# Gate and up of 18 of 22 feed-forward blocks as seven half-size block products, in a two-layer decoder trunk

## The chip, the cores and the metric

One Trainium2 chip, of which the kernel uses one core. The metric is the device time of one execution in microseconds (us), the median of several runs. PE is TensorE, PEld its weight load, DVE is VectorE, ACT is ScalarE, POOL is GpSimd, SP is SyncE.

## The reference

Two layers work on 544 positions at once (512 of a prompt and 8 samples of 4), model width 1024. Each layer has a mixer of four head groups (delta rule, short convolution, window attention, chunked token mixing) and then a feed-forward part of width 2816. Only the latter is touched by the change:

```python
x = x + jnp.concatenate([out_a, out_b, out_c, out_d], axis=-1) @ p['w_out']
h2 = rmsnorm(x, p['norm2_g'])
gate, f_conv_new = causal_dwconv(st['f_conv'], h2 @ p['ffn_w_gate'], p['ffn_conv_w'])
x = x + (jax.nn.silu(gate) * (h2 @ p['ffn_w_up'])) @ p['ffn_w_down']
```

The convolution runs over positions, width 3, each channel by itself. All is in float32.

## The kernel before

Activations lie with channels on the 128 partitions and the 544 positions along the free axis, so a tile of 128 channels is 128x544; `HT` is 272, half of the positions. Each float32 product is made of three: every operand is split into a high part, rounded to TensorE's fp32r format, and a low part, the remainder, and `gemm` (before L652) issues hi x hi, hi x lo, lo x hi for each of the k blocks of 128 channels, each for both halves of the positions: 6 matmuls of 128x272 for each block of 128x128 weights. TensorE's order is the program's own, which an `Order` object with side generators (the mixers) lays out; the other engines' queues are filled by a scheduler, earlier program text first among what is ready.

Weights come by `weights()` in the order of their use. `wload` issues the DMA of one weight tile (512 KB) on SP's queue into one of 2 buffers (`wrp`), `wprep` splits it: ScalarE copies the high part (L641), VectorE subtracts for the low part (L643), into 3 buffers each. `wnext` keeps three split tiles ready before it hands one out, so a tile is split when the buffer of the one three earlier has been given back by TensorE.

The feed-forward part (from L1553) goes through 22 blocks of 128 hidden channels, in groups of 6, 6, 6 and 4. In a block the gate product runs over the 8 k blocks (48 matmuls into PSUM tile `pgt`), then the up product (48 into `pup`); both take `xs`, the split of x times the norm's weight, which isn't yet divided by the root mean square. `rstd`, the reciprocal of that root, comes from the norm's own matmuls (`nps`) in the middle of the first up product, and multiplies the results: L1576 and L1577 on VectorE for the gate (into `pbf`, the buffer of the convolution), L1584 on GpSimd for the silu output `sl`. Then the convolution (`conv`: one ScalarE pass L694, two VectorE passes L696 into `cacc`), silu on ScalarE (L1582, L1583), the product with `pup` on VectorE (L1590), and the split into `hdh` and `hdl` (L499, L500). GpSimd also copies state in and out (`sfo`, L1578, L1579; L689). At the end of a group 8 down products (`pdn`, 36 matmuls in a group of 6, 24 in one of 4) take the group's hidden tiles, and VectorE adds each to the residual `xr` (L1600). The last two down products of the last layer are made half by half in `finale` (`pdl`), where each weight tile serves one half at a time.

```python
for wi, x in ((0, xh), (0, xl), (1, xh)):
    ...
    for j in range(2):
        mm(p[:, P0 + HT * j:P0 + HT * j + HT], w, x[:, HT * j:HT * j + HT],
           start=first, stop=last)
```

## Time and profile before

| | |
|---|---|
| median of 3 runs | 1376.19 us (1376.03 to 1376.20) |
| the profiled execution | 1375.83 us, of which the span from first to last instruction 1374.0 us |
| TensorE busy | 1343.9 us (98%), 12982 matmuls |
| VectorE, ScalarE, GpSimd busy | 777.2, 515.2, 292.2 us (57%, 37%, 21%) |
| granted TensorE clock | 0.99 |

The time outside the span is 1.8 us. Matmul spans overlap in the records, so the distance from one matmul to the next is read from a chain of many, not from one span.

### The profile page before, as it was taken

What the parts mean: (1) busy time and instruction counts of PE and PEld (TensorE: products, weight loads), DVE (VectorE), ACT (ScalarE), POOL (GpSimd) and SP (SyncE); (2) the same over time, 40 slices, a digit from 0 to 9 for tenths busy, and PEclk for the clock granted to TensorE, in tenths of its full rate; (3) what the DMA queues carried; (4) which work ended last, traced back from release to release, by engine and by line L of the source; (5) the groups of instructions that cost most, each with busy time, mean ns of one, the idle gap of its engine ahead of it and who ended that gap; (6) DMA issues with size and microseconds to landing.
All of it is one profiled execution on the core that took longest, in us unless ns stands there. A gap on an engine that the chain in (4) does not pass through costs nothing.

```text
span 1374.0 us, 30046 instructions
## 1 busy us (share of the span) xinstructions
PE 1343.9 (98%) x12982; PEld 1299.8 (95%) x12982; DVE 777.2 (57%) x1319; ACT 515.2 (37%) x852; POOL 292.2 (21%) x466
## 2 busy tenths in 40 slices
PE   8899999999999999999998999999999999999997
PEld 7888888999999999999998888989999999999997
DVE  5897944665445445435658977537444444444446
ACT  5446324443223223313534353335432332232234
POOL 2431220032103102203124311202320230121121
PEclk9899999999999999999999999999999999999999
DMA  6222241232232232232432222413223232322323
GB/s 224 89 83 72 82 133 43 82 113 77 81 106 79 76 107 80 74 106 67 140 120 79 78 82 62 138 52 87 92 81 89 93 85 80 98 89 71 103 68 96
DMA packets 48084, 125.62 MB, mean 91 GB/s; under 512 B 10144, under 2 KB 14432, under 8 KB 47824
## 3 DMA queue, kind: packets, MB, share of 16 engines
q1 hardware_dynamic: 47952, 123.70, 29.6%
q8 instruction: 102, 1.67, 0.5%
q14 instruction: 30, 0.25, 0.1%
HBM read 115.01 MB, written 8.67 MB: 90 GB/s over the span
## 4 chain that ended last, share of the span: by engine, by line
PE 88%; DVE 8%; issue 2%; ACT 1%; DMA 0%; DVEq 0%; SPq 0%; ACTq 0%
PE pup L417 19%; PE pgt L417 19%; PE pdn L417 19%; PE po L417 7%; PE ptm L417 2%; PE pj_b L417 2%; PE pj_z L417 2%; PE pj_u L417 2%; PE pj_h L417 2%; PE pj_cq L417 2%; PE pj_c L417 2%; PE p L417 2%; PE pj_v L417 1%; DVE wl L643 1%; DVE cacc L696 1%
## 5 line engine op out<-in xcount | busy, mean ns | idle before, releaser
L641 ACT ACTIVATE wh<-wr 128x1024 fp32r<-128x1024 f32 (+3 forms) x218 | 208.5, 957 | 502.0 <-PE pdn L417 177.2
L643 DVE TENSOR_TENSOR wl<-wr,wh 128x1024 fp32r<-128x1024 f32 (+3 forms) x218 | 246.2, 1129 | 24.2 <-ACT wh L641 18.3
L417 PE MATMUL pgt<-xl,wh 128*128 128x272 f32 x704 | 146.7, 290 | 0.0
L417 PE MATMUL pup<-xl,wh 128*128 128x272 f32 x704 | 146.7, 290 | 0.0
L417 PE MATMUL pup<-xh,wl 128*128 128x272 f32 x704 | 145.9, 289 | 0.0
L417 PE MATMUL pgt<-xh,wl 128*128 128x272 f32 x704 | 145.9, 289 | 0.0
L417 PE MATMUL pup<-xh,wh 128*128 128x272 f32 x704 | 145.9, 288 | 0.0
L417 PE MATMUL pgt<-xh,wh 128*128 128x272 f32 x704 | 145.9, 288 | 0.0
L417 PE MATMUL pdn<-hdl,wh 128*128 128x272 f32 x688 | 142.8, 289 | 0.0
L417 PE MATMUL pdn<-hdh,wh 128*128 128x272 f32 x688 | 142.4, 288 | 0.0
L417 PE MATMUL pdn<-hdh,wl 128*128 128x272 f32 x688 | 142.2, 288 | 0.0
L1600 DVE TENSOR_TENSOR xr<-xr,pdn 128x544 f32<-128x544 f32 x62 | 44.7, 721 | 142.0 <-PE pdn L417 141.8
L1578 POOL COPY sfo<-pbf 128x2 f32<-128x2 f32 x44 | 14.8, 336 | 517.9 <-DVE pbf L1576 517.9
L1576 DVE TENSOR_TENSOR pbf<-pgt,rstd 128x512 f32<-128x512 f32 x44 | 30.5, 693 | 148.3 <-PE pgt L417 142.9
L417 PEld LDWEIGHTS pgt<-xh,wh 128*128 128x128 f32 x704 | 110.8, 188 | 0.0
L417 PEld LDWEIGHTS pup<-xh,wh 128*128 128x128 f32 x704 | 110.8, 188 | 0.0
L417 PEld LDWEIGHTS pup<-xl,wh 128*128 128x128 f32 x704 | 110.7, 189 | 0.0
L417 PEld LDWEIGHTS pgt<-xl,wh 128*128 128x128 f32 x704 | 110.7, 189 | 0.0
L417 PEld LDWEIGHTS pgt<-xh,wl 128*128 128x128 f32 x704 | 110.7, 188 | 0.0
L417 PEld LDWEIGHTS pup<-xh,wl 128*128 128x128 f32 x704 | 110.7, 188 | 0.0
L417 PEld LDWEIGHTS pdn<-hdl,wh 128*128 128x128 f32 x688 | 108.1, 188 | 0.1
L417 PEld LDWEIGHTS pdn<-hdh,wl 128*128 128x128 f32 x688 | 108.1, 188 | 0.0
(523 smaller groups left out, 2680.0 us busy)
## 6 DMA issues: line engine op xcount, KB each, us to landing
wr<-w_g SPq DMA_DIRECT2D x44, 512.0 KB
wr<-w_u SPq DMA_DIRECT2D x44, 512.0 KB
wr<-w_ch SPq DMA_DIRECT2D x38, 512.0 KB
wr<-w_d SPq DMA_DIRECT2D x48, 384.0 KB
wr<-w_o SPq DMA_DIRECT2D x12, 384.0 KB
wr<-w_d SPq DMA_DIRECT2D x16, 256.0 KB
xr<-x_in SPq DMA_DIRECT2D x7, 544.0 KB
wr<-w_tm SPq DMA_DIRECT2D x8, 392.0 KB
```

The lines of the kernel that those rows point to most:

```text
L417: nc.tensor.matmul(out, lhsT, rhs, **kw)
L641: act(hi, r, AF.Copy)
L643: tt(lo, r, hi.bitcast(F32), op=ALU.subtract)
L696: stt(acc[:, 0:out_n], pb[:, j:j + out_n], wcol[:, j:j + 1], acc[:, 0:out_n], op0=ALU.mult, op1=ALU.add)
L1576: tt(pb[:, 2:2 + SEQ], pflat(p, 0, SEQ), rstd[:, 0:SEQ], op=ALU.mult)
L1578: pool.tensor_copy(sfo[:, f, 0:2], pb[:, SEQ:SEQ + 2])
L1600: tt(xk(m), xk(m), pflat(p), op=ALU.add)
```

## The change

The 1024 input channels and the 544 positions are each cut in half, and the gate and up weights are taken as the two rows of a 2x2 block matrix. The product of a 2x2 block matrix (gate and up by the two halves of the channels) with a 2x2 block matrix (the two halves of the channels by the two halves of the positions) is made from seven block products in place of eight, with sums of blocks on both sides. Each block product runs over 4 k blocks, in the same three terms, one half of the positions: 12 matmuls of 128x272 (`chain`).

- Sums of weights: `wsums`, four GpSimd additions of 128x512 for each hidden block, in two tiles `s12` and `s43`. The tiles to split are then gate, `s12`, `s43` (1024 wide each) and the second half of up (512 wide). Four raw weight buffers in place of two, plus two for the sums.
- Sums of activations: `Forms`. `halves` makes the normed input (x times weight times `rstd`) and splits its halves; `sums` makes and splits the four sums. Both are made once in each layer.
- Blocks 0 and 1 stay as they were (`raw`); blocks 2 and 3 are plain products on the split normed input (`plain`), where ScalarE copies the gate to `pbf` with no factor; blocks 4 to 21 are made by `seven`. Only `raw` still multiplies by `rstd`.
- In `seven` partial results stay in PSUM across chains: a chain with start=False adds to what ScalarE has copied out to `sn` before.
- Groups are 4, 6, 6, 6, and the down products of a group are spread among the blocks of the next one (after the blocks of a group of six: 2, 2, 2, 1, 1, 0); those of the last group follow at the end.
- The pools `hlp`, `lv`, `px` and `pyy` become one pool of 51 buffers.

```diff
-FGROUPS = [(0, 6), (6, 12), (12, 18), (18, 22)]
+FGROUPS = [(0, 4), (4, 10), (10, 16), (16, 22)]
+RAW, PLAIN = 2, 4
...
+def _ffn_order():
+    o, todo = [], []
+    for f0, f1 in FGROUPS:
+        n = f1 - f0
+        for j, f in enumerate(range(f0, f1)):
+            o.append(("plain" if f < PLAIN else "seven", f, f0, f1))
+            k = -(-len(todo) // max(n - 1 - j, 1))
+            o += todo[:k]
+            todo = todo[k:]
+        o += todo
+        todo = [("down", m, f0, f1) for m in range(NK)]
+    return o + todo
...
+FFN_ORDER = _ffn_order()
...
-    hlp = ctx.enter_context(tc.tile_pool(name="hlp", bufs=28))
-    wrp = ctx.enter_context(tc.tile_pool(name="wrp", bufs=2))
+    slabs = ctx.enter_context(tc.tile_pool(name="slabs", bufs=51))
+    wrp = ctx.enter_context(tc.tile_pool(name="wrp", bufs=4))
+    wsp = ctx.enter_context(tc.tile_pool(name="wsp", bufs=2))
     whp = ctx.enter_context(tc.tile_pool(name="whp", bufs=3))
     wlp = ctx.enter_context(tc.tile_pool(name="wlp", bufs=3))
     p5 = ctx.enter_context(tc.tile_pool(name="p5", bufs=6))
-    lv = ctx.enter_context(tc.tile_pool(name="lv", bufs=1))
     pd = ctx.enter_context(tc.tile_pool(name="pd", bufs=5))
-    px = ctx.enter_context(tc.tile_pool(name="px", bufs=16))
-    pyy = ctx.enter_context(tc.tile_pool(name="pyy", bufs=5))
     pc = ctx.enter_context(tc.tile_pool(name="pc", bufs=7))
...
+    class Forms:
...
+        def __init__(self, src):
+            self.src, self.got, self.h = src, [], []
+            self.hv = [slice(HT * i, HT * i + HT) for i in range(2)]
+        def halves(self, kp):
+            h = []
+            for k in (kp, kp + NK // 2):
+                x, g = self.src(k)
+                t = nx("hn", [128, T])
+                stt(t, x, g, rstd, op0=ALU.mult, op1=ALU.mult)
+                h.append(t)
+            j = kp % 2
+            if j == 0:
+                self.pk = [[nx(f"f{i}" + c, [128, T], F32R) for c in "hl"] for i in "12"]
+            c_ = slice(HT * j, HT * j + HT)
+            one = []
+            for (hi, lo), v in zip(self.pk, (h[0][:, 0:HT], h[0][:, HT:T])):
+                act(hi[:, c_], v, AF.Copy)
+                tt(lo[:, c_], v, hi[:, c_].bitcast(F32), op=ALU.subtract)
+                one.append((hi[:, c_], lo[:, c_]))
+            sb = split(h[1], "f3")
+            self.got.append(one + [(sb[0][:, s], sb[1][:, s]) for s in self.hv])
+            self.h.append(h)
+        def sums(self, kp):
+            h, self.h[kp] = self.h[kp], None
+            (b11, b12), (b21, b22) = ((t[:, 0:HT], t[:, HT:T]) for t in h)
+            u, v = n5("fu", T), n5("fv", T)
+            n1, n2, t3, n4 = u[:, 0:HT], u[:, HT:T], v[:, 0:HT], v[:, HT:T]
+            tt(n1, b11, b12, op=ALU.subtract)
+            stt(n2, n1, -1.0, b22, op0=ALU.mult, op1=ALU.subtract)
+            tt(t3, b22, b12, op=ALU.subtract)
+            tt(n4, b21, n2, op=ALU.add)
+            for t in (split(u, "f4"), split(v, "f5")):
+                self.got[kp] += [(t[0][:, s], t[1][:, s]) for s in self.hv]
...
+        def whole(self):
+            return [(kp + NK // 2 * i, g[2 * i:2 * i + 2]) for kp, g in enumerate(self.got) for i in range(2)]
+        def parts(self):
+            return [[g[i] for g in self.got] for i in (0, 2, 3, 4, 5, 6, 7)]
+    def chain(o, wt, k0, xs, start=True):
+        hi, lo = wt
+        n = len(xs)
+        for k in range(n):
+            xh, xl = xs[k]
+            for i, (w, x) in enumerate(((hi, xh), (hi, xl), (lo, xh))):
+                mm(o, w[:, k0 + k, :], x, start=start and k == 0 and i == 0, stop=k == n - 1 and i == 2,
+                   skip_group_check=not start)
+            yield 0.0
...
+            for kind, i, f0, f1 in FFN_ORDER:
+                if kind == "down":
+                    yield I["w_d"][l, i, :, f0:f1], f1 - f0, 128
+                elif kind == "plain":
+                    yield I["w_g"][l, i], NK, 128
+                    yield I["w_u"][l, i], NK, 128
+                else:
+                    yield I["w_g"][l, i], I["w_u"][l, i]
...
+    wload_, wsplit_, wready = [], [], []
...
-            wload_.append(r)
+            wload_.append([wraw(*x)] if len(x) == 3 else [wraw(src, NK, 128) for src in x])
+    def wsums(g, u):
+        K = NK // 2
+        lo_, hi_ = slice(0, K), slice(K, NK)
+        s12 = wsp.tile([128, NK, 128], F32, tag="ws", name="s12")
+        s43 = wsp.tile([128, NK, 128], F32, tag="ws", name="s43")
+        add = pool.tensor_tensor
+        add(s12[:, lo_], u[:, lo_], u[:, hi_], op=ALU.add)
+        add(s12[:, hi_], g[:, lo_], s12[:, lo_], op=ALU.add)
+        add(s43[:, lo_], g[:, hi_], s12[:, hi_], op=ALU.add)
+        add(s43[:, hi_], g[:, lo_], u[:, lo_], op=ALU.add)
+        return [g, s12, s43, u[:, hi_]]
...
+        if not wsplit_:
+            if not wload_:
+                wload()
+            if not wload_:
+                return
+            rs_ = wload_.pop(0)
+            wsplit_.extend(rs_ if len(rs_) == 1 else wsums(*rs_))
+        r = wsplit_.pop(0)
...
+    def gemm_halves(p, wt, xs):
+        for n, (k, x) in enumerate(xs):
+            for i, (w, c) in enumerate(((0, 0), (0, 1), (1, 0))):
+                for j in range(2):
+                    mm(p[:, P0 + HT * j:P0 + HT * j + HT], wt[w][:, k, :], x[j][c],
+                       start=n == 0 and i == 0, stop=n == NK - 1 and i == 2)
+            if n < NK - 1:
                 yield 0.0
...
+            hid = {}
+            fm = Forms(lambda k: (xk(k), P(l, "n2g", k, k + 1)))
...
+            def raw(f, first):
+                p = psmm("pgt")
+                yield from gemm(p, wnext(), xs)
+                pu = psmm("pup")
...
+                pool.tensor_tensor(sl, sl, rstd, op=ALU.mult)
+                yield 0.0
+                yield from gu
+                tt(sl, sl, pflat(pu), op=ALU.mult)
+                hid[f] = split(sl, "hd")
+                yield 0.0
...
+            def plain(f):
+                p = psmm("pgt")
+                yield from gemm_halves(p, wnext(), fm.whole())
+                pb, dec = gate_in(f)
+                act(pb[:, 2:2 + SEQ], pflat(p, 0, SEQ), AF.Copy)
+                act(dec[:, :, 2:6], bs(pflat(p, SEQ, T)), AF.Copy)
+                sl = gate_out(f, pb, dec)
+                yield 0.0
+                pu = psmm("pup")
+                yield from gemm_halves(pu, wnext(), fm.whole())
+                tt(sl, sl, pflat(pu), op=ALU.mult)
+                hid[f] = split(sl, "hd")
+                yield 0.0
+            def seven(f):
...
+                B11, B21, B22, N1, N2, T3, N4 = fm.parts()
+                K = NK // 2
+                a_ = ps("pA", [128, HT])
+                b_ = psa.tile([128, HT], F32, tag="pa1", name="pB")
+                d_ = psa.tile([128, HT], F32, tag="pa0", name="pD")
+                sn = pd.tile([128, 4, HT], F32, tag="d5", name="sn")
+                pb, dec = gate_in(f)
+                n = SEQ - HT
+                w = wnext()
+                yield from chain(a_, w, 0, B11)
+                act(sn[:, 0], a_, AF.Copy)
+                yield from chain(b_, w, K, B21)
+                tt(pb[:, 2:2 + HT], b_, sn[:, 0], op=ALU.add)
+                w = wnext()
+                yield from chain(d_, w, 0, N1)
+                act(sn[:, 1], d_, AF.Copy)
+                yield from chain(a_, w, K, N2, start=False)
+                act(sn[:, 2], a_, AF.Copy)
+                w = wnext()
+                yield from chain(d_, w, 0, B22, start=False)
+                tt(pb[:, 2 + HT:2 + SEQ], d_[:, 0:n], sn[:, 2, 0:n], op=ALU.add)
+                tt(dec[:, :, 2:6], bs(d_[:, n:HT]), bs(sn[:, 2, n:HT]), op=ALU.add)
+                sl = gate_out(f, pb, dec)
+                yield from chain(a_, w, K, T3, start=False)
+                act(sn[:, 3], a_, AF.Copy)
+                up = n5("up", T)
+                stt(up[:, HT:T], a_, -1.0, sn[:, 1], op0=ALU.mult, op1=ALU.subtract)
+                c_ = psmm("pC")[:, 0:HT]
+                yield from chain(c_, wnext(), 0, N4)
+                tt(up[:, 0:HT], c_, sn[:, 3], op=ALU.subtract)
+                tt(sl, sl, up, op=ALU.mult)
+                hid[f] = split(sl, "hd")
+                yield 0.0
...
+            for kind, i, f0, f1 in FFN_ORDER:
+                if kind == "plain":
+                    yield from raw(i, i == 0) if i < RAW else plain(i)
+                    if i == 0:
+                        for kp in range(NK // 2):
+                            fm.halves(kp)
+                    elif i < 3:
+                        fm.sums(2 * i - 2)
+                        fm.sums(2 * i - 1)
+                    continue
+                if kind == "seven":
+                    yield from seven(i)
+                    continue
+                m, last = i, f1 == NF
+                hd = [hid[f] for f in range(f0, f1)]
+                if last and l + 1 == depth and m >= NK - 2:
...
+                p = psmm("pdn")
+                yield from gemm(p, wnext(), hd)
+                tt(xk(m), xk(m), pflat(p), op=ALU.add)
...
+    nc = _bacc.Bacc("TRN2", target_bir_lowering=False, num_devices=1, dynamic_dma_scratch_size=512)
```

## Rows read from the trace of the kernel before

**Rows 1.** The page, part 1: busy us, share of the span, instructions.
```profile
PE 1343.9 (98%) x12982; PEld 1299.8 (95%) x12982; DVE 777.2 (57%) x1319; ACT 515.2 (37%) x852; POOL 292.2 (21%) x466
```

**Rows 2.** The page, part 4: shares of the chain that ended last.
```profile
PE 88%; DVE 8%; issue 2%; ACT 1%; DMA 0%; DVEq 0%; SPq 0%; ACTq 0%
```

**Rows 3.** The chain that ended last, in time: start us, us, what.
```profile
285.35 6.08 PE pgt L417 x48
...
297.97 6.08 PE pgt L417 x48
...
358.77 36.37 PE pdn L417 x288
...
1357.46 4.53 PE pdl L417 x36
```

**Rows 4.** Busy time in stretches: length, each engine, then granted clock, DMA.
```profile
285.30:334.40 49.10, 49.10 (x390) 49.10 (x389) 25.06 (x33) 20.90 (x31) 15.84 (x22) 1.00 0.27 92
...
1012.60:1339.00 326.40, 326.40 (x2593) 326.40 (x2592) 147.37 (x192) 96.51 (x132) 59.81 (x88) 1.00 0.29 85
```

**Rows 5.** VectorE groups by form: busy us, mean ns, idle before.
```profile
L643 DVE TENSOR_TENSOR wl<-wr,wh 128x1024 fp32r<-128x1024 f32 x132 | 167.9, 1272 | 19.8 <-ACT wh L641 13.9
...
L696 DVE SCALAR_TENSOR_TENSOR cacc<-pbf,prm,cacc 128x560 f32<-128x560 f32 x88 | 70.4, 800 | 4.0 <-ACT cacc L694 2.3
...
L643 DVE TENSOR_TENSOR wl<-wr,wh 128x768 fp32r<-128x768 f32 x60 | 57.1, 951 | 0.0
...
L1590 DVE TENSOR_TENSOR sl<-sl,pup 128x544 f32<-128x544 f32 x44 | 31.8, 722 | 111.0 <-PE pup L417 103.1 <-POOL sl L1584 7.9
...
L500 DVE TENSOR_TENSOR hdl<-sl,hdh 128x544 fp32r<-128x544 f32 x44 | 31.6, 719 | 0.5
...
L643 DVE TENSOR_TENSOR wl<-wr,wh 128x512 fp32r<-128x512 f32 x18 | 12.3, 684 | 0.0
```

**Rows 6.** VectorE instructions of line 547 and of line 596: min/median/max ns.
```profile
L547 DVE SCALAR_TENSOR_TENSOR xl<-xr,prm,xh x32: 772/784/1886, 5.5 to 965.8; 128x544 fp32r<-128x544 f32 x32
...
L596 DVE TENSOR_TENSOR sq<-sq x2: 439/441/443, 1361.1 to 1363.0; 128x272 f32<-128x272 f32 x2
```

**Rows 7.** Timeline of VectorE, gate and up of layer 0.
```profile
296.47 0.69 DVE L1576 TENSOR_TENSOR pbf<-pgt,rstd 128x512 f32<-128x512 f32 x1 [2.73 <-ACT rstd L541]
```

**Rows 8.** ScalarE groups by form.
```profile
L641 ACT ACTIVATE wh<-wr 128x1024 fp32r<-128x1024 f32 x132 | 139.6, 1058 | 313.9 <-PE pgt L417 142.1 <-PE pdn L417 63.9 <-PE pup L417 27.3
...
L641 ACT ACTIVATE wh<-wr 128x512 fp32r<-128x512 f32 x18 | 11.4, 632 | 26.6 <-PE pgt L417 8.7 <-PE pup L417 6.2 <-PE pdn L417 5.7
...
L1253 ACT ACTIVATE oc<-pov 128x256 f32<-128x256 f32 x8 | 3.0, 380 | 6.0 <-PE pov L417 6.0
```

**Rows 9.** GpSimd instructions of four lines: min/median/max ns.
```profile
L841 POOL TENSOR_TENSOR Gu<-cst,gg x4: 1043/1046/1046, 61.6 to 789.0; 128x512 f32<-128x512 f32 x4
...
L1102 POOL TENSOR_TENSOR s<-s,ex x4: 1045/1544/1917, 165.0 to 835.6; 128x512 f32<-128x512 f32 x4
...
L1579 POOL COPY sfo<-pbf x44: 190/1243/1250, 297.3 to 1334.6; 128x16 f32<-128x16 f32 x44
...
L1584 POOL TENSOR_TENSOR sl<-sl,rstd x44: 1354/1359/1367, 301.1 to 1337.4; 128x544 f32<-128x544 f32 x44
```

**Rows 10.** Timelines of VectorE and of GpSimd at 511 us.
```profile
511.31 1.23 DVE L643 TENSOR_TENSOR wl<-wr,wh 128x1024 fp32r<-128x1024 f32 x1
...
511.35 1.24 POOL L1579 COPY sfo<-pbf 128x16 f32<-128x16 f32 x1
```

**Rows 11.** Busy time in stretches of 2 us, layer 1.
```profile
726.00:728.00 2.00, 0.00 (x0) 0.00 (x0) 1.97 (x8) 0.24 (x1) 0.05 (x1) 1.00 0.19 68
...
728.00:730.00 2.00, 0.00 (x0) 0.00 (x0) 1.94 (x6) 1.73 (x4) 1.46 (x5) 0.65 0.00 0
...
732.00:734.00 2.00, 2.00 (x10) 2.00 (x11) 2.00 (x5) 0.02 (x1) 0.00 (x0) 0.50 0.66 172
```

More of the change, by code (lines that the diff above doesn't have):

```diff
@@ L451, in n5, with nx @@
         return p5.tile([128, w], F32, tag="w5", name=nm)
-    def nx(nm, shape):
-        return px.tile(shape, F32, tag="x5", name=nm)
+    def nx(nm, shape, dt=F32):
+        return slabs.tile(shape, dt, tag="s5", name=nm)
     def ncc(nm, shape):
@@ L459, in ny @@
     def ny(nm, shape):
-        return pyy.tile(shape, F32, tag="y5", name=nm)
+        return nx(nm, shape)
     def ps(nm, shape):
@@ L615, in weights, with wraw @@
                 yield I["w_o3"][l, m], NK, 128
-            for f0, f1 in FGROUPS:
-                for f in range(f0, f1):
-                    yield I["w_g"][l, f], NK, 128
-                    yield I["w_u"][l, f], NK, 128
-                for m in range(NK):
-                    yield I["w_d"][l, m, :, f0:f1], f1 - f0, 128
-    wgen = weights()
-    wload_, wready = [], []
+            for kind, i, f0, f1 in FFN_ORDER:
[6 more added lines that the diff above has]
+                    yield I["w_g"][l, i], I["w_u"][l, i]
+    wgen = weights()
+    wload_, wsplit_, wready = [], [], []
+    def wraw(src, nk, w):
+        r = wrp.tile([128, nk, w], F32, tag="wr", name="wr")
+        nc.sync.dma_start(r, src)
+        return r
     def wload():
@@ L786, in gates @@
         L.beta, L.nbeta, L.gg, L.ex, L.bec = beta, nbeta, gg, ex, bec
-        L.oT = [lv.tile([128, T], F32, tag=f"oT{pr}", name=f"oT{pr}") for pr in range(2)]
+        L.oT = [nx(f"oT{pr}", [128, T]) for pr in range(2)]
         od.mark(f"gates{l}", 1.0)
     def halves(x):
-        h = hlp.tile([128, SEQ], F32R, tag="hl", name="hvh")
-        lo = hlp.tile([128, SEQ], F32R, tag="hl", name="hvl")
+        h, lo = nx("hvh", [128, SEQ], F32R), nx("hvl", [128, SEQ], F32R)
         act(h, x, AF.Copy)
@@ new lines, in main, with gate_in, gate_out @@
+            hid = {}
+            fm = Forms(lambda k: (xk(k), P(l, "n2g", k, k + 1)))
+            def gate_in(f):
+                pb = n5("pbf")
+                return pb, conv_in(pb, 3, stf[:, f])
+            def gate_out(f, pb, dec):
+                pool.tensor_copy(sfo[:, f, 0:2], pb[:, SEQ:SEQ + 2])
+                pool.tensor_copy(sfo[:, f, 2:18].rearrange("p (b s) -> p b s", b=DB), dec[:, :, 4:6])
+                acc, accd = conv(pb, 3, P(l, "fcw", 3 * f, 3 * f + 3), 560)
+                sl = n5("sl", T)
+                act(sl[:, 0:SEQ], acc[:, 0:SEQ], AF.Silu)
+                act(bs(sl[:, SEQ:T]), accd, AF.Silu)
+                return sl
@@ new lines, in raw @@
+            def raw(f, first):
+                p = psmm("pgt")
+                yield from gemm(p, wnext(), xs)
+                pu = psmm("pup")
+                gu = gemm(pu, wnext(), xs)
+                if first:
+                    for _ in range(4):
+                        yield next(gu)
+                    nrm.finish()
+                pb, dec = gate_in(f)
+                tt(pb[:, 2:2 + SEQ], pflat(p, 0, SEQ), rstd[:, 0:SEQ], op=ALU.mult)
+                tt(dec[:, :, 2:6], bs(pflat(p, SEQ, T)), bs(rstd[:, SEQ:T]), op=ALU.mult)
+                sl = gate_out(f, pb, dec)
[5 more added lines that the diff above has]
+                yield 0.0
@@ new lines, in main @@
+            for kind, i, f0, f1 in FFN_ORDER:
[14 more added lines that the diff above has]
+                if last and l + 1 == depth and m >= NK - 2:
+                    if m == NK - 2:
+                        yield from finale(xk, xr, nnrm, hd)
+                    continue
+                p = psmm("pdn")
+                yield from gemm(p, wnext(), hd)
+                tt(xk(m), xk(m), pflat(p), op=ALU.add)
+                if last:
+                    if l + 1 < depth:
+                        nx_xs.append(xsplit(xk(m), P(l + 1, "n1g", m, m + 1)))
+                    nnrm.feed(m, xk(m))
+                    if l + 1 == depth:
+                        act(xk(m), xk(m), AF.Copy, scale=fng[:, m:m + 1])
+                yield 0.0
```

67 lines of the change are left out of this document (6 added, 61 removed).

## The prediction

> **What bounds the kernel now.** I read the page's busy table first [rows 1]: TensorE is busy 98% of the span, VectorE 57%, ScalarE 37%, GpSimd 21%. Then the shares of the chain that ended last [rows 2]: PE 88%, VectorE 8%. So the kernel is a queue of matmuls, with its gaps elsewhere. Then the same chain in time [rows 3], to see what the feed-forward part is made of: 48 matmuls of a gate or an up product stand as one piece of 6.08 us, the next piece begins where the last one ended, and 288 matmuls of the down products take 36.37 us. There is no wait between them. The stretches agree [rows 4]: from 285.3 to 334.4 us (four blocks at the start of layer 0) and from 1012.6 to 1339.0 us (most of layer 1's part) TensorE is busy for all of the time at granted clock 1.00, and VectorE for 51% and 45% of it. What matters is therefore how many matmuls there are, how far apart they stand, and whether the other engines, which get more work, still keep ahead.
>
> **Matmuls removed.** A block costs 96 matmuls now; seven chains of 12 make 84. That is 12 less in 18 blocks of 2 layers: 432. A piece of 48 gives 6.08/48 = 126.7 ns from one to the next. The new chains use a weight tile for one half of the positions at a time, which the gate and up products never do, but the last two down products do: 36 in 4.53 us are 125.8 ns [rows 3], so this form costs no more. At 126.2 ns, 432 matmuls are **54.5 us**. Blocks 0 to 3, the down products and the norms keep their counts, and regrouping the downs moves them without changing their number. From here all other terms are losses, for whatever hides work cannot shorten a queue that has no gap.
>
> **Steady blocks: the load.** TensorE has 84 x 126.2 ns = 10.6 us for a block. VectorE: the weight tiles to split become 3.5 of the 1024 kind for 2, that is 3 x 1.23 [rows 10] + 0.68 [rows 5] = 4.4 us; the two convolution passes 1.6; product and hidden split 1.44 [rows 5]; and four half-width additions from PSUM, taken as 0.44 each by the nearest row [rows 6], 1.8: together 9.2 us. GpSimd: four additions of 128x512, 1.05 us each when nothing is in the way and up to 1.92 [rows 9], 4.2 us; three small copies at 0.19, 0.6; the 1.36 us product with `rstd` falls away. ScalarE gains 1.06 + 0.63 for splits and 4 copies from PSUM at about 0.38 [rows 8], 3.2 us a block, on a queue that is 30% busy here [rows 4]; hidden. Over a group of six with its 8 downs, TensorE has 6 x 10.6 + 36.4 = 100 us, VectorE 6 x 9.2 + 8 x (0.95 + 0.72) = 69 us, GpSimd 29 us. On average both fit.
>
> **Where the two collide.** In the timelines a GpSimd copy of 128x16 begins 0.04 us after a VectorE split of 1.23 us and ends 0.05 us after it [rows 10]; alone such a copy takes 0.19 us, and 1.24 is its median [rows 9]. So a GpSimd operation that reads SBUF waits out a VectorE operation with two SBUF inputs; line 547's maximum of 1.89 us against a median of 0.78 [rows 6] is the same thing the other way round. The Trainium skill (SBUF — State Buffer, Who interferes with whom) says that the two fully exclude each other for a whole instruction, which speaks against putting the sums on GpSimd. By that rule the losses below stand at their upper ends, some 46 us in all, and without it near their lower ones; the trace agrees with the rule in the rows just named.
>
> If nothing overlaps, a group needs 69 + 29 = 98 us of 100. But the downs are not spread evenly: the last block of a group has none behind it, and the first of the next has none ahead, so twice a layer two blocks stand together: 21.2 us of TensorE against 2 x 9.2 (full overlap) to 2 x (9.2 + 4.8) = 28.0 us (none). On top come the splits of up to three hidden blocks (3 x 0.72 = 2.2 us): the 51 buffers less 32 for the forms of the input and 2 for states leave 17, so from the third block of a group the hidden tiles wait for the old group's last down. Two weight tiles are split ahead, of 24 matmuls or 3.0 us each; one of them I count as cover. Bounds for each of the 4 places: 0 to 28.0 + 2.2 - 21.2 - 3.0 = 6.0 us. I take 1.5, near the lower end, since half-width operations with a PSUM input can run beside GpSimd: **6 us** in all.
>
> **The start of each feed-forward part.** `rstd` arrives about 11.2 us after the first gate product starts (296.47 against 285.35 [rows 7, 3]). Only then can VectorE make the forms: for each of 4 pairs, two scalings at 0.78, two half-width subtractions at 0.44, one of 0.72 [rows 5, 6], 3.16 us, 12.6 in all; and four sums at 0.44 and two subtractions at 0.72, 3.2 us, 12.8 in all. They are due when block 2 and the third chain of block 4 start, at 24.8 and 52.1 us. VectorE is busy 25 of the first 49 us today [rows 4], 4.7 of it before `rstd` (one addition 0.72, two splits 2.46, two low parts 0.78 and 0.72); two gate scalings go to ScalarE (1.7 less). So after `rstd` it has 25.1 - 4.7 - 1.7 + 25.4 = 44 us of work in 41. GpSimd adds its 2 x 1.36, 4.2 of sums and eight copies at 0.19, 8.4 us, all in the way if nothing overlaps. Loss for a layer: 0 (the operations can be a little closer than their spans) to 3 + 8 = 11 us; I take 5, between them, as VectorE's queue has no room to catch up here: **10 us** in two layers. Queued behind the forms on VectorE are the splits of block 2's weights and the scaling of block 1's gate, which gives back the PSUM tile that block 2 needs; so the wait will show at block 2 and block 4.
>
> **Waits inside a block.** The third chain's tile (D) is copied out by ScalarE while the fourth chain runs, 12 matmuls or 1.51 us, before the fifth adds to it; likewise A between its second and third use. The copy is 0.38, so 1.1 us is left for what stands ahead of it. One split (1.06) just fits; two would hold TensorE by 1.0 us. Bounds 0 to 1.0 at each of two places; I take 0.03, as the queue is free two thirds of the time: **2 us** over 36 blocks. `sn` has one buffer (four of five hold `xr`); its writer waits for the last addition of the block before, with 3 us in hand.
>
> **At nothing.** Weight loads: SP issues two at a time into four buffers, the same bytes, at a DMA share of 0.29 [rows 4]. What is queued behind them on SP are only loads that are due later. The longer last down products (36 in place of 24 matmuls) give the norm of the next layer more cover, not less. The common pool can let a mixer run earlier or wait; nothing in the trace prices it, bounds plus or minus 2 us, 0 taken.
>
> **The sum.** The profiled execution took 1375.83 us, its span 1374.0; 1374.0 - 54.5 + 10 + 6 + 2 = 1337.5, with 1.8 outside it 1339.3. The median is 0.4 above that execution: **1339.7 us**.
>
> **Rivals.** (a) *Clean.* VectorE's slack holds and the forms come in time: losses up to 7 us, 1321.7 to 1328. For it: VectorE idles over half of these stretches. Against: the 44 us in 41 after `rstd`. Chance 0.2. (b) *The forecast*, waits at the starts and at group ends, 1328 to 1352: 0.52. (c) *GpSimd and VectorE shut each other out all through*: starts at 11, ends at 6.0, 22 + 24 = 46 us, so 1368; with part of it, or a little beyond, 1352 to 1372. It is the rule of the Trainium skill's page SBUF — State Buffer, Who interferes with whom, taken at its word. For it the copy that waited out the split; against it the room in blocks with downs. Chance 0.2. (d) *Slower*: the copies of D and A reach ScalarE's queue behind a split that itself waits for GpSimd's sums, so TensorE stops twice in each block. At the 1.0 us bound this is 36 x 2 x 1.0 = 72 us, 1394; from 0.76 us a place it outweighs the 54.5. A stop of that kind can also cost the clock: after TensorE did nothing from 726 to 730 us the granted clock read 0.50, the lower of its two levels, until after 734 [rows 11]. Against it: the sums have a whole block's time, and ScalarE is 30% busy. Chance 0.08 with (e), no measurable change, at 0.02. That the matmuls would not fall in number is excluded by the count, and that they would stand further apart by the row of the last down products [rows 3].
>
> **How the numbers follow.** Most likely is (b) at its sum, 1339.7. The range 1324 to 1364 leaves out about 0.05 of (a) at its floor, 0.06 of (c), and (d) and (e). About 0.2% (2.8 us) is what a measurement of this kernel can tell from no change. Faster 0.92, within it 0.02, slower 0.06.
>
> **What would show it.** Right: pieces of 12 matmuls at 1.51 us in the chain; 432 fewer matmuls; waits of TensorE on VectorE of a few us at block 2 and block 4 of each layer, and next to none in blocks followed by downs. GpSimd's additions nearer to 2 us than to 1.05 would point to (c). Wrong: waits at each fifth or sixth chain on ScalarE (d), a granted clock under 1.00 in the feed-forward part, or chains of 12 longer than 1.55 us with no wait.

## The result and the profile after

| | before | after |
|---|---|---|
| median | 1376.2 us (1376.03 to 1376.67, 4 runs) | 1356.46 us (1354.94 to 1357.27, 4 runs) |
| profiled execution | 1375.83 us, span 1374.0 | 1355.9 us, span 1353.6 |

The ratio is 0.9855, 95% interval 0.9838 to 0.9872: faster, by 19.7 us where 36.5 were forecast. First the busy table and the shares of the chain that ended last (parts 1 and 4 of the page of the changed kernel, against [rows 1, 2]):

```profile
PE 1297.3 (96%) x12550; PEld 1247.8 (92%) x12550; DVE 994.2 (73%) x1579; ACT 638.2 (47%) x1116; POOL 459.6 (34%) x570
...
PE 79%; DVE 14%; ACT 3%; issue 3%; DMA 1%; DVEq 0%; SPq 0%; ACTq 0%
```

TensorE has 12982 - 12550 = 432 matmuls less, as counted. VectorE's share of the chain went from 8% to 14%: the matmuls that are left wait for it. Where, the chain in time shows (start us, us, what; against [rows 3]):

```profile
283.04 6.01 PE pgt L436 x48
...
312.23 3.43 DVE hn L578 x2
...
325.17 2.76 PE pgt L436 x10
327.93 7.03 PE pup L436 x48
334.96 6.00 PE pgt L436 x48
...
348.45 1.51 PE pB L436 x12
...
446.96 2.24 DVE wl L736
...
450.05 4.74 PE pdn L436 x36
```

From the first gate of layer 0 (283.04) to the gate of block 3 (334.96) are 51.92 us; the 292 matmuls between them need 36.7 at the spacing of the undisturbed pieces (125.6 ns). In layer 1 the same stretch takes 51.84. So some 15 us are lost in each layer in one place: block 2, the first block that reads the normed halves; block 4, where the prediction looked for waits too, has none to speak of. The waits of TensorE say for what (us in total, times, longest; the whole span):

```profile
PE pgt L436 <- DVE f1l L587: 16.1, 6, 6.0
...
PE pdn L436 <- DVE up L1743: 4.1, 6, 1.2
PE pgt L436 <- ACT f1h L586: 2.6, 2, 1.4
```

`f1l`, and below `f3l`, are low parts of halves. VectorE's timeline of layer 0 (start us, us; only the rows that matter) shows why `f1l` is late:

```profile
294.06 0.69 DVE L1687 TENSOR_TENSOR pbf<-pgt,rstd 128x512 f32<-128x512 f32 x1 [2.62 <-ACT rstd L557]
...
302.99 1.48 DVE L578 SCALAR_TENSOR_TENSOR hn<-xr,prm,rstd 128x544 f32<-128x544 f32 x2
...
312.15 3.51 DVE L578 SCALAR_TENSOR_TENSOR hn<-xr,prm,rstd 128x544 f32<-128x544 f32 x2
315.59 1.50 DVE L598 TENSOR_TENSOR fu<-hn 128x272 f32<-128x272 f32 x1
317.01 1.56 DVE L600 TENSOR_TENSOR fv<-hn 128x272 f32<-128x272 f32 x1
318.49 0.43 DVE L598 TENSOR_TENSOR fu<-hn 128x272 f32<-128x272 f32 x1
318.85 1.49 DVE L600 TENSOR_TENSOR fv<-hn 128x272 f32<-128x272 f32 x1
...
320.89 0.43 DVE L587 TENSOR_TENSOR f1l<-hn,f1h 128x272 fp32r<-128x272 f32 x1
...
325.74 0.71 DVE L516 TENSOR_TENSOR f3l<-hn,f3h 128x544 fp32r<-128x544 f32 x1
```

Two things stand there. The first pair of halves starts 8.9 us after `rstd` came, behind block 0's convolution, a weight split, block 0's product and block 1's gate. And the same pair takes 1.48 us once and 3.51 another time, a sum 0.43 or 1.50. What GpSimd did in those microseconds:

```profile
310.81 2.56 POOL L717 TENSOR_TENSOR s<-wr 128x512 f32<-128x512 f32 x1 [6.99 <-DMA wr<-w_u]
313.33 1.75 POOL L720 TENSOR_TENSOR s<-wr 128x512 f32<-128x512 f32 x1
315.04 1.75 POOL L718 TENSOR_TENSOR s<-wr,s 128x512 f32<-128x512 f32 x1
316.75 1.52 POOL L1690 TENSOR_TENSOR sl<-sl,rstd 128x544 f32<-128x544 f32 x1
...
318.58 1.46 POOL L719 TENSOR_TENSOR s<-wr,s 128x512 f32<-128x512 f32 x1
```

All but the product with `rstd` are the sums of block 4's weights, due some 30 us later; alone such an addition takes 1.05 us [rows 9]. The slow instructions of the two engines lie beside each other. Last the clock, in stretches of 4 us (length, then busy time of PE, PEld, DVE, ACT, POOL, the granted clock, DMA share, GB/s):

```profile
312.00:316.00 4.00, 1.97 (x11) 1.41 (x9) 4.00 (x4) 1.05 (x3) 4.00 (x3) 0.62 0.20 61
316.00:320.00 4.00, 0.00 (x0) 0.00 (x0) 4.00 (x4) 0.35 (x1) 4.00 (x5) 0.50 0.00 0
320.00:324.00 4.00, 2.62 (x11) 2.50 (x11) 4.00 (x9) 0.61 (x2) 0.04 (x1) 0.50 0.00 0
324.00:328.00 4.00, 3.62 (x15) 3.22 (x15) 4.00 (x10) 3.42 (x7) 0.00 (x0) 0.50 0.00 0
```

VectorE is busy all the time and TensorE stops; the granted clock falls to 0.50 (1.2 GHz), and stays there until 330 us, after the last wait. In the chain above, the 48 matmuls of block 2's up product then take 7.03 us against 6.00 (6.87 in layer 1): 1.0 and 0.9 us are the clock's. The 10 before them take 2.76 us against 1.26, but some of them also wait for `f3l`, which VectorE ends at 326.45, so only a part of that 1.5 us is the clock's.

### The profile page after: what moved, and what is told of

Same layout as the page of the kernel before. It is cut to its first block, busy times and chain, and to the rows that moved or that the text cites. A ratio compares the mean times of both kernels' runs of the same rounds, so it can differ in the third digit from the quotient of the medians.

```text
span 1353.6 us, 29982 instructions
## 1 busy us (share of the span) xinstructions
PE 1297.3 (96%) x12550; PEld 1247.8 (92%) x12550; DVE 994.2 (73%) x1579; ACT 638.2 (47%) x1116; POOL 459.6 (34%) x570
## 4 chain that ended last, share of the span: by engine, by line
PE 79%; DVE 14%; ACT 3%; issue 3%; DMA 1%; DVEq 0%; SPq 0%; ACTq 0%
PE pdn L436 16%; PE pA L436 11%; PE pD L436 7%; PE po L436 7%; PE pB L436 4%; PE pup L436 4%; DVE wl L736 3%; PE pC L436 3%; PE pgt L436 3%; PE ptm L436 2%; PE pj_b L436 2%; PE pj_cq L436 2%; PE pj_z L436 2%; PE pj_h L436 2%; PE pj_c L436 2%
## 5 line engine op out<-in xcount | busy, mean ns | idle before, releaser
L736 DVE TENSOR_TENSOR wl<-wr,wh 128x768 fp32r<-128x768 f32 (+3 forms) x218 | 267.5, 1227 | 68.8 <-ACT wh L734 67.4
L734 ACT ACTIVATE wh<-wr 128x768 fp32r<-128x768 f32 (+3 forms) x218 | 193.1, 886 | 186.9 <-PE pA L436 32.8
L717 POOL TENSOR_TENSOR s<-wr 128x512 f32<-128x512 f32 x36 | 53.5, 1487 | 229.9 <-DMA wr<-w_u 140.8
L734 ACT ACTIVATE wh<-s 128x1024 fp32r<-128x1024 f32 x72 | 76.2, 1059 | 93.8 <-PE pdn L436 69.3
L436 PEld LDWEIGHTS pdn<-hdh,wh 128*128 128x128 f32 x680 | 106.5, 188 | 8.1 <-issue 3.9
L736 DVE TENSOR_TENSOR wl<-s,wh 128x1024 fp32r<-128x1024 f32 x72 | 101.8, 1414 | 7.1 <-ACT wh L734 7.0
L798 DVE SCALAR_TENSOR_TENSOR cacc<-pbf,prm,cacc 128x560 f32<-128x560 f32 x88 | 78.6, 894 | 34.8 <-ACT cacc L796 34.0
L718 POOL TENSOR_TENSOR s<-wr,s 128x512 f32<-128x512 f32 x36 | 65.3, 1813 | 1.3
L720 POOL TENSOR_TENSOR s<-wr 128x512 f32<-128x512 f32 x36 | 62.1, 1725 | 0.0
L719 POOL TENSOR_TENSOR s<-wr,s 128x512 f32<-128x512 f32 x36 | 59.2, 1645 | 5.7 <-DVE wl L736 4.9
L436 PE MATMUL pA<-f5h,wh 128*128 128x272 f32 x144 | 41.7, 289 | 0.0
L436 PE MATMUL pB<-f3h,wl 128*128 128x272 f32 x144 | 41.6, 289 | 0.0
```

What stands on the lines that cost most here:

```text
L436: nc.tensor.matmul(out, lhsT, rhs, **kw)
L717: add(s12[:, lo_], u[:, lo_], u[:, hi_], op=ALU.add)
L718: add(s12[:, hi_], g[:, lo_], s12[:, lo_], op=ALU.add)
L719: add(s43[:, lo_], g[:, hi_], s12[:, hi_], op=ALU.add)
L720: add(s43[:, hi_], g[:, lo_], u[:, lo_], op=ALU.add)
L734: act(hi, r, AF.Copy)
```

## The experiments

To compare the runs I counted the matmuls in TensorE's timeline from the first gate of a feed-forward part, and took from the time of the nth what n of them need at 125.55 ns. The difference is what had been lost by then. "Start" is n = 580 (blocks 0 to 3, block 4 with the two down products behind it, and most of block 5); "rest" is from there to the last matmul of the last down products. Where in a matmul its time is taken moves a start by 0.1 to 0.4 us.

| run | ratio to before, interval | start, layer 0 / 1 | rest, layer 0 / 1 |
|---|---|---|---|
| the change | 0.9855, 0.9838 to 0.9872 | 15.3 / 15.3 us | 4.6 / 5.0 us |
| weight sums held | 0.9793, 0.9776 to 0.9809 | 11.3 / 11.8 | 3.8 / 5.4 |
| input sums late | 0.9797, 0.9782 to 0.9811 | 10.6 / 11.1 | 4.6 / 4.9 |
| both | 0.9797, 0.9781 to 0.9812 | 11.5 / 11.7 | 4.7 / 4.1 |
| no weight sums | 0.9729, 0.9715 to 0.9744 | 9.4 / 11.6 | 0.7 / 1.6 |
| halves first | 0.9763, 0.9749 to 0.9778 | 9.3 / 9.5 | 3.6 / 4.0 |
| halves first, held, late | 0.9763, 0.9748 to 0.9778 | 9.3 / 9.0 | 4.5 / 3.5 |
| halves first, late, no weight sums | 0.9649, 0.9633 to 0.9665 | 4.4 / 4.3 | 0.9 / 1.7 |
| three blocks, held | 0.9797, 0.9782 to 0.9812 | 8.3 / 10.2 | 6.0 / 4.3 |
| three blocks, held, halves first | 0.9739, 0.9722 to 0.9755 | 6.5 / 6.5 | 3.6 / 4.0 |
| three blocks, held, late, one pair first | 0.9742, 0.9728 to 0.9757 | 6.6 / 6.7 | 4.1 / 4.5 |
| the same, weight sums on VectorE | 0.9748, 0.9734 to 0.9761 | 5.6 / 5.8 | 8.0 / 6.0 |

The runs with three blocks have 12 matmuls more in each layer, 1.5 us, which the table doesn't count as lost.

**Weight sums held.** In the first seven-product block of a layer a one-column copy of the last low part goes ahead of GpSimd's sums, which are issued behind it (`issue_after` queues what it encloses behind the instruction named; `wadds` holds the four additions):

```diff
+        if form_end:
+            t = pool.tensor_copy(s12[:, 0, 0:1], form_end.pop().bitcast(F32)[:, 0:1])
+            with tc.issue_after(t.ins):
+                wadds(g, u, s12, s43)
...
```

> GpSimd's weight sums of the first seven-product block of each layer are held until the last low part of the forms is written, so GpSimd is idle of them while VectorE forms the halves. Sharing theory: the doubled VectorE operations (hn pair 3.51 us, fu and fv some 1.5 us each) fall back to their time alone, the last low part comes 4 to 6 us earlier in each layer, the clock fall is shorter, and the time falls by 8 to 16 us, to 1340 to 1348. Too-much-work theory (VectorE simply has more to do than the plain blocks cover): 0 to 3 us, 1353 to 1357. Queue-order theory (the forms' own sums stand ahead of the low parts): 0 to 4 us, since the order stays. If the held sums then come too late for block 4, TensorE waits there instead and the time rises.

Measured 1346.97 us, some 8.5 less than the change (0.0062 of 1376): the lower end of what the sharing theory asked. In the timelines of VectorE and of GpSimd:

```profile
312.44 2.57 DVE L580 SCALAR_TENSOR_TENSOR hn<-xr,prm,rstd 128x544 f32<-128x544 f32 x2
...
314.93 0.43 DVE L604 TENSOR_TENSOR fu<-hn 128x272 f32<-128x272 f32 x1
...
316.97 0.43 DVE L589 TENSOR_TENSOR f1l<-hn,f1h 128x272 fp32r<-128x272 f32 x1
```

```profile
310.98 2.75 POOL L1707 TENSOR_TENSOR sl<-sl,rstd 128x544 f32<-128x544 f32 x1 [6.87 <-ACT sl L1691]
```

The sums `fu` are back at 0.43, and the low part that came at 320.89 comes at 316.97. The pair of halves is still at 2.57, beside GpSimd's product with `rstd`. Block 2 loses 9.5 in place of 15.4 us; 1.8 and 2.2 us went again in block 3 and at a down product behind block 4, for GpSimd made its sums from 326.84 on, beside the sums of the inputs, which took 1.53 there. (The copy itself, of one column, took 4.29 us beside VectorE's full queue, from 322.58, so the sums came later than was meant.)

**Input sums late.** Order on VectorE alone:

```diff
...
-                        fm.sums(2 * i - 2)
-                        fm.sums(2 * i - 1)
+                        with tc.issue_after(fm.end.ins):
+                            fm.sums(2 * i - 2)
+                            fm.sums(2 * i - 1)
```

> Only the order on VectorE changes: the forms' sums fu and fv are put behind the last low part of the halves; GpSimd's weight sums stay where they are. Queue-order theory: the low part of halves 2 no longer stands behind 5 us of sums, block 2 ends 4 to 5 us earlier in each layer, 8 to 12 us in all, 1344 to 1349. Sharing theory: the halves are still stretched, 2 to 6 us in all, 1350 to 1355. Too-much-work theory: the sums only come later and block 4 waits for them instead, 0 to 2 us either way.

Measured 1347.38 us, 8.0 less: what the queue-order theory asked, though GpSimd's sums ran where they had. **Both together** was to tell whether the two add up:

> Both edits: the weight sums held until the last low part, the forms' sums behind the last low part. Sharing and queue order together: each wait of block 2 for a low part shrinks to what 8 half rounds of VectorE take, 12 to 24 us less, 1332 to 1344. Too-much-work theory: block 2 is shorter but block 4 waits for its sums of inputs and of weights, both now late: 0 to 4 us, and by as much slower if both gather behind the last low part.

Measured 1346.78 us: they don't. Block 2 lost only 6.9 and 7.1 us, but block 3 another 4.6, most of it in a new wait of TensorE:

```profile
PE pup L436 <- DVE sl L1725: 5.7, 2, 2.9
```

The sums of both kinds were now pushed into the same few microseconds behind the halves. This is near what the too-much-work theory had said (it had block 4 wait, not block 3, and at most 4 us of gain where 8 came), so at this point it stood. **No weight sums** should have settled it. The four additions are left out and the products use unsummed weights, so this run prices the sums and is no version of the kernel:

```diff
...
-        return [g, s12, s43, u[:, hi_]]
+        return [g, g, u, u[:, hi_]]
```

> Leaves out the sums of weights on GpSimd (products 2 to 6 of a block use unsummed weights), everything else as in the changed kernel. This prices those sums wherever they act: the sharing during the forms, the longer weight splits (1414 ns against 1220 alone), and their wait. Sharing theory: as much as holding them brings (8 to 16 us) and some 4 to 8 us more at the group ends, 1334 to 1346. Too-much-work theory: 4 to 8 us from the group ends alone, 1348 to 1352. Queue-order theory: 2 to 8 us.

Measured 1337.85 us, 17.3 less and inside what the sharing theory asked. Outside the start the loss fell from 4.6 and 5.0 to 0.7 and 1.6 us, and VectorE's busy time from 994.2 to 915.7 with the same 1579 instructions:

```profile
PE 1294.8 (97%) x12550; PEld 1246.3 (93%) x12550; DVE 915.7 (68%) x1579; ACT 637.0 (48%) x1116; POOL 187.6 (14%) x426
```

So 144 additions on GpSimd had cost VectorE 78.5 us, 0.55 us each. But at the start 9.4 and 11.6 us stayed, as with everything else tried so far. The 2.1 us between its two layers are a price of the clock: the waits are the same (the longest 1.7 us in both), but behind them, at the same distance from the first gate, layer 0 was back at full clock and layer 1 was not:

```profile
322.00:326.00 4.00, 3.91 (x30) 3.69 (x30) 4.00 (x7) 3.80 (x8) 0.52 (x1) 1.00 0.00 0
981.40:985.40 4.00, 4.00 (x19) 4.00 (x19) 4.00 (x7) 3.43 (x7) 0.03 (x1) 0.50 0.01 2
```

Two readings were left: VectorE has some 9 us too much work there, or its order alone does as much harm as the sharing.

**Halves first.** The four pairs are issued right behind the scaling of block 0's gate:

```diff
+                if first:
+                    for kp in range(NK // 2):
+                        fm.halves(kp)
                 sl = gate_out(f, pb, dec)
...
```

> Only the order: the four halves are issued right after the first block's gate is normed, ahead of its convolution, its up product and the second block's gate; weight sums and cover as in the changed kernel. Order theory: the first halves start some 8 us earlier, the low parts are there before GpSimd's weight sums begin, block 2 loses 0 to 6 us instead of 15.3 in each layer: 18 to 30 us less, 1326 to 1338. Too-much-work theory: the convolutions and splits that now stand behind the halves are late in their turn (second block's gate, weights), 0 to 8 us less, 1347 to 1356.

Measured 1343.16 us: 12.7 less, between the two forecasts. The first pair now starts at 294.57, but the fourth falls under GpSimd's sums:

```profile
294.57 1.47 DVE L578 SCALAR_TENSOR_TENSOR hn<-xr,prm,rstd 128x544 f32<-128x544 f32 x2
...
312.47 3.59 DVE L578 SCALAR_TENSOR_TENSOR hn<-xr,prm,rstd 128x544 f32<-128x544 f32 x2
```

**Halves first, weight sums held, input sums late.**

> The halves first, the forms' own sums behind the last low part, and the weight sums held until then. Order theory: like the run with the halves first or up to 6 us better, 1324 to 1336, since nothing shares VectorE's operands any more and the sums of inputs still have block 2 and 3 as cover. Too-much-work theory: as the run with both edits but no earlier halves, 1343 to 1349.

Measured 1342.9 us, no better; the too-much-work theory was nearer (1343 to 1349). Of 9.3 us in layer 0, 3.9 are lost in block 1, whose gate is scaled behind a pair of halves, the rest in block 3.

**Halves first, input sums late, no weight sums** takes both away at once, and tells the two readings apart:

> Leaves out the sums of weights on GpSimd (products 2 to 6 of a block use unsummed weights); halves first and the forms' own sums behind the last low part, as in the run with halves first and both edits. So far a loss of 9 to 11 us per layer has stayed in the first 580 matmuls of each feed-forward part whatever was taken away alone. Sharing theory (what is left there is VectorE's order and GpSimd's access, each hiding the other): with both gone 1 to 4 us per layer stay, 10 to 15 us less than the run without the sums alone, and with 3 us per layer saved at the group ends 1322 to 1328. Too-much-work theory (VectorE has some 9 us more to do than the matmuls cover, whoever shares): 8 to 10 us per layer stay, 1334 to 1338, as the run without the sums alone.

Measured 1327.41 us. The start loses 4.4 and 4.3 us, the rest 0.9 and 1.7. The waits that were left at the start are one of 1.9 us in block 1 of each layer and one of 1.2 (us in total, times, longest):

```profile
PE pup L436 <- DVE pbf L1686: 3.8, 2, 1.9
...
PE pgt L436 <- DVE f3l L592: 1.2, 1, 1.2
```

So the too-much-work theory falls, and the four runs make a square of the loss at the start (layer 0 / 1): 15.3 / 15.3 as changed; 9.4 / 11.6 without the weight sums; 9.3 / 9.0 in the better order; 4.4 / 4.3 with both. The order is worth 5 to 7 us of it, the sums 4 to 6 (layer 1's figures with the 2.1 us of clock above in them; in the third of the four the weight sums are held as well). What the 4.4 us that stay are is not shown. They are not all VectorE's own work: in layer 0 its queue there still holds a pair of halves and a low part stretched by some 2.3 us together (1.47 and 0.43 alone), beside GpSimd's two products with `rstd`:

```profile
300.59 2.60 DVE L579 SCALAR_TENSOR_TENSOR hn<-xr,prm,rstd 128x544 f32<-128x544 f32 x2
...
313.83 1.63 DVE L588 TENSOR_TENSOR f1l<-hn,f1h 128x272 fp32r<-128x272 f32 x1
```

**Three blocks on the un-normed split**, which gives 12.1 us more of cover (the weight sums are held here as well):

```diff
-RAW, PLAIN = 2, 4
+RAW, PLAIN = 3, 5
...
```

> One block more runs on the un-normed split (12.1 us of matmuls of cover more per layer between the norm and the first use of the halves), one seven-product block becomes plain (12 matmuls, 1.5 us per layer more); weight sums held until the last low part as in the hold run. Too-much-work theory (after holding, 9.5 us per layer are still lost in the first block that reads the halves because VectorE has too little time before it): these 9.5 us go to 0 to 2, so 15 to 19 us less than the hold run and 3 us more for the matmuls: 1330 to 1335. Order theory (the halves are late because other work stands before them on VectorE): the same, since 12 us more hide any order. If the held sums now make the first seven-product block wait, it comes back there: 1338 to 1345.

Measured 1347.38 us, a miss for all that was forecast: 8.3 and 10.2 us stay. The wait has only moved:

```profile
PE pup L436 <- DVE sl L1710: 8.5, 3, 3.3
```

The products that give back the covering blocks' PSUM tiles stand behind the halves in VectorE's queue. More cover helps only if the short work of the covering blocks comes through.

> Three blocks on the un-normed split, weight sums held, halves first. Where the three-block run already has all its halves in time, the order adds nothing: within 2 us of it. If it still waits there, this is better by what it still loses, 1328 to 1333.

With the halves first as well: 1339.2 us. Against the held run with two blocks, the third block alone brought nothing (1346.97 and 1347.38); the new order on top of it brought 8.2 us, not the 14 to 19 that were asked, for 6.5 us are still lost at each start.

> Three blocks on the un-normed split, weight sums held, the forms' own sums last, and only the first pair of halves moved ahead of the first block's convolution. The run with three blocks and all halves first still loses 6.5 us per layer: 2.1 to 3.6 at the second block's up product, behind a pair of halves, the rest at the first seven-product block. Order theory: the first part goes, 4 to 5 us less than that run, 1333 to 1336. Too-much-work theory: the loss only moves to the plain blocks, 1337 to 1341; the forms' sums, now last, may make the first seven-product block wait 3 us more per layer, up to 1345.

With one pair first and the input sums late: 1339.89 us, inside the forecast of the too-much-work theory for this run. The loss in block 1 fell from 2.1 and 3.6 to 1.2 and 1.4 us, but as much was lost in the plain blocks (5.4 and 5.5 by matmul 388, against 5.2 and 5.5): it moved. Both versions beat the changed kernel and the kernel before; between them no difference can be told.

**Matmuls in the wait.** To price the clock, 56 matmuls into a PSUM tile that nothing reads stand where TensorE waits 6.0 us:

```diff
...
+                    for _ in range(56):
+                        nc.tensor.matmul(dm, w[0][:, 0, :], fm.got[0][0][0], start=True, stop=True)
```

> The changed kernel with 56 matmuls more in each layer, whose results are not read, placed where TensorE waits 6.0 us for the low part of halves 2 in the first plain block (56 at 126 ns are 7.0 us, inside the wait of 1.42 + 6.00 us). Clock theory: TensorE works through the wait, the granted clock stays at or near 1.00 instead of 0.50 from 314 to 330 us, the some 22 to 34 matmuls after the wait take 126 in place of 227 ns each, 2 to 3.4 us per layer, 1350 to 1352. Without it: the low parts bound the block on their own, within 1 us of the changed kernel, 1354 to 1357; if the clock has fallen before the added matmuls begin, they take up to 12.7 us and the time rises by up to 5 us per layer.

Measured 1353.39 us, ratio 0.9837 (0.9823 to 0.9852), which overlaps the changed kernel's: inconclusive. The stretches of layer 0 show why:

```profile
312.00:316.00 4.00, 4.00 (x22) 4.00 (x21) 4.00 (x4) 1.21 (x3) 4.00 (x3) 0.57 0.18 59
316.00:320.00 4.00, 4.00 (x34) 4.00 (x33) 4.00 (x4) 0.20 (x1) 3.98 (x5) 1.00 0.00 0
320.00:324.00 4.00, 3.52 (x25) 3.06 (x24) 4.00 (x9) 0.67 (x2) 0.00 (x0) 1.00 0.00 0
324.00:328.00 4.00, 3.42 (x15) 2.80 (x15) 4.00 (x9) 4.00 (x8) 0.00 (x0) 0.73 0.00 0
```

The clock had fallen before the added matmuls began, came back to 1.00 with them, and fell again in the shorter waits behind them. In layer 1 it stood at 1.00 from 976 to 988 us, all through the added matmuls, and fell behind them (0.50 from 992 to 996). The up product of block 2 starts 44.81 us after the first gate in layer 0, against 44.85: the low parts set that time, with the clock at 1.00 or at 0.50 ahead of it. What half clock costs is seen better in the run with no weight sums: 2.1 us in one layer.

**The sums on VectorE.** The last run asks what it would cost to give GpSimd's additions to the engine that they disturb. The kernel is the one with one pair first, but for this line, and the sums are not held back any more:

```diff
...
-        add = pool.tensor_tensor
+        add = dve.tensor_tensor
```

> As the run with three blocks on the un-normed split, one pair of halves first and the forms' own sums last, but the four sums of weights of each seven-product block are made on VectorE in place of GpSimd (and are not held). On VectorE they should take about 0.68 to 0.69 us each, as its other operations on 128x512, 2.6 us per block; on GpSimd they take 1.5 to 1.8 us each, and VectorE's splits beside them are stretched by about as much. Sharing theory (what costs is the time in which the two shut each other out, not VectorE's count of work): little changes or it gets better, from 3 us slower to 8 us faster than that run, 1332 to 1343, the splits of summed weights back at 1.23 us. Load theory (VectorE has no room for 2.6 us more in blocks of 10.6 us without downs): 2 to 4 us are lost at each of 4 group ends in each layer beyond what is lost now, 1348 to 1370.

Measured 1341.34 us (5 runs), against 1339.89 with the sums on GpSimd: no difference that can be told. The busy tables, first with the sums on GpSimd, then on VectorE:

```profile
PE 1293.6 (97%) x12574; PEld 1246.0 (93%) x12574; DVE 982.3 (73%) x1569; ACT 630.9 (47%) x1104; POOL 460.9 (34%) x566
```

```profile
PE 1294.6 (97%) x12574; PEld 1246.5 (93%) x12574; DVE 983.2 (73%) x1705; ACT 630.5 (47%) x1104; POOL 227.8 (17%) x428
```

VectorE is busy 982.3 us without the 136 additions and 983.2 with them. The groups of splits and of sums, in the same order (busy us, mean ns):

```profile
L753 DVE TENSOR_TENSOR wl<-s,wh 128x1024 fp32r<-128x1024 f32 x68 | 97.2, 1429 | 4.3 <-ACT wh L751 3.8
...
L736 POOL TENSOR_TENSOR s<-wr,s 128x512 f32<-128x512 f32 x34 | 64.4, 1895 | 1.3
```

```profile
L742 DVE TENSOR_TENSOR wl<-s,wh 128x1024 fp32r<-128x1024 f32 x68 | 83.0, 1220 | 4.3 <-ACT wh L740 2.4
...
L724 DVE TENSOR_TENSOR s<-wr,s 128x512 f32<-128x512 f32 x34 | 23.3, 684 | 0.1
```

An addition takes 684 ns on VectorE, and the split of summed weights 1220 in place of 1429. The load theory was right in part: 6.3 and 3.6 us were lost between matmuls 580 and 1200, at down products behind blocks 5 and 6 and inside block 10 (layer 0's chain has a weight load of 4.28 us ahead of the first, which came late), but only 1.7 and 2.4 after that, against 3.8 and 4.6 with the sums on GpSimd. The wait inside block 10, once in each layer, is one for a ScalarE copy of A, which no other run shows:

```profile
PE pA L436 <- ACT sn L1732: 2.1, 2, 1.1
```

## Why the prediction was right or wrong

The sign, the count of matmuls and the place were right, and the time lies in the range; the saving is little more than half of the forecast one, and 1356.5 us belongs to the interval of rival (c), not to that of the forecast (1328 to 1352). That it is in the range owes something to luck: the starts lost three times what was taken for them, and a gain that was not forecast made up for part. Of the signs named, the chains of 1.51 us, the count and the waits at block 2 came, those at block 4 did not; against the forecast came a granted clock under 1.00 and GpSimd's additions of 1.49 to 1.81 us in the mean, nearer to 2 than to 1.05, which were to point to (c).

*Matmuls removed.* 432, and chains of 12 stand in the chain as 1.51 us: right. Not forecast: matmuls that are not changed stand a little closer too, 48 in 6.00 to 6.05 us against 6.08 [rows 3], and layer 0's part took 126.5 ns a matmul before (401.2 us for 3172), layer 1's 126.2 (400.6 for 3175), against 125.55 now where nothing waits: on the 5912 matmuls that are left 4.6 us are gained. Why stays open.

*The start of each feed-forward part.* This is the step that failed: 5 us forecast, bounds 0 and 11, measured 15.3. The count of work itself ("44 us of work in 41", 3 us short) is near the 4.4 us that stay with order and sums out of the way, but its 41 us end at block 4 and the 4.4 are lost in blocks 1 to 3, part of them to what is left of the sharing: that the two agree is chance. Three things were missing. First, the order: I counted VectorE as working on the forms from `rstd` on, and compared sums of work with one late due time. In the queue 8.9 us lay between `rstd` and the first pair, 3.3 of them idle, and the input sums stood ahead of low parts that TensorE waited for; 5 to 7 us. Second, the sharing: I had it in the bound (8.4 us of GpSimd's work in the way) and took 5 of 11, with no reason why it would mostly overlap. GpSimd made block 4's sums as soon as their weights came, inside those very microseconds; 4 to 6 us. Third, the clock: 1.0 and 0.9 us of it, and a part of another 1.5, are matmuls at half clock, which I had priced only for rival (d). So the upper bound was no bound.

*Two blocks standing together.* 6 us forecast in 4 places of 1.5. Measured are five steps in layer 0 and four in layer 1, of 0.7 to 1.4 us; before three of them in each layer the chain has a blocked split of 2.24 us, as above. Only four of the nine stand behind two blocks without downs between them (matmuls 1204 and 1996 of each layer), 4.3 us where 6 were forecast; the others are at downs behind blocks 12 and 18 and at the last downs. In all it is 9.6 us. The size of a step was right, their places and number not. Without the weight sums only the step at a layer's last downs stays, 1.0 to 1.3 us; so most of this loss comes from the sums too.

*Waits inside a block.* 2 us forecast; no wait of TensorE for the copies of D and A stands in the trace of the change. Rival (d) is wrong for it; with the sums on VectorE such a wait came once in each layer, 1.1 us.

*The sum.* 54.5 for the matmuls and 4.6 for the spacing, less 30.6 at the starts and 9.6 elsewhere, are 18.9; the two spans differ by 20.4. The other 1.5 lies outside the feed-forward parts, the first of which begins 2.3 us earlier (283.04 against 285.35 us).

*Rival (c)* had the right mechanism and 0.2. The Trainium skill (SBUF — State Buffer, Who interferes with whom) says that GpSimd and VectorE exclude each other for whole instructions when the one reads SBUF and the other has two SBUF inputs. The runs agree with the rule, in the 982.3 against 983.2 us above. The prediction named it as speaking against the change, with rows that agreed, and then took values below the middle of its bounds. Where (c) overshot is the room in blocks with downs, which did absorb most of it, as the forecast said: some 5 us were lost in each layer's rest, not 12; at the starts it fell short, 11 where 15.3 were lost.

## What to carry to other kernels

An elementwise operation given to GpSimd was no free work here: 136 additions there stretched VectorE by as much as making them itself took, so count such operations in VectorE's time before believing that they lie beside it. For a stretch that begins with a late operand, compare not work with cover but the queue with each due time: what stands ahead of the first piece that TensorE needs, and what was put between the pieces. And when single repairs each give 8 us and together no more, test the pair with the suspected cause taken out altogether before concluding that the work is too much.

## What the runs showed that was not expected

That the exchange is so even: 92.4 us of stretching (stretched VectorE work 982.3, less 983.2 - 93.3 of its own) for 226.6 us of GpSimd's time, against 93.3 us of additions on VectorE; this takes the rest of VectorE's work to be the same in the two runs. Operations that read PSUM were not stretched: the half-width addition to `up` stands at 431 ns in the changed kernel and at 433 in the run with no weight sums. Of its 36 in the changed kernel, the 10 that lie almost wholly beside a GpSimd operation on two tensors take 428 ns in the mean, the 18 that lie beside none 434:

```profile
L1740 DVE SCALAR_TENSOR_TENSOR up<-pA,sn 128x272 f32<-128x272 f32 x36 | 15.5, 431 | 0.0
```

```profile
L1732 DVE SCALAR_TENSOR_TENSOR up<-pA,sn 128x272 f32<-128x272 f32 x36 | 15.6, 433 | 0.0
```

And that the clock fell behind waits as short as 1.7 us, but not behind each of them. In the changed kernel the granted clock is 0.98 from 312 to 313 us, with TensorE busy, and 0.50 from 313 to 314: behind a wait of 1.71 us that ended at 311.3, and before the long one of 6.0 began. In the run with added matmuls it fell in layer 0 behind that same wait, and in layer 1 behind a wait of 1.70 us it did not; in the run with the halves first, late and no weight sums it fell in layer 0 behind a wait of 1.9 us (0.57 from 304 to 308 us) and not in layer 1. So the cost of a short wait has to be read for each place from the granted clock behind it.
